# Hybrid RWKV-7 / S5 block: a 16-row RWKV inverse, readout of block 3 in halves, GLU of three blocks behind a norm

## Chip, cores and metric

One core of a Trainium2 chip runs the whole layer in one launch. The metric is the device time in microseconds; less is better. Engines are called PE (TensorE), DVE (VectorE), ACT (ScalarE), POOL (GpSimd) and SP (the queue that issues the DMAs here).

## What is computed

One layer over 2048 latent tokens and 256 context tokens, width 1024, all in float32. After an RMSNorm with modulation, one projection gives the inputs of two mixers: a bidirectional RWKV-7 (8 heads of 64) and a bidirectional diagonal S5 with a gated output (GLU). Their outputs are joined, projected, added to x; a second norm, a SwiGLU FFN (2816 wide) and a final norm follow. The recurrence of one RWKV head and direction is

```
sa    = state @ (-kk_t)
state = state * w_t + sa (kk_t * a_t)^T + v_t k_t^T
y_t   = state @ r_t
```

and the S5 output is `z * sigmoid(z @ glu_w + glu_b)` with `z = gelu(y)`. Context is scanned first, in each direction, and its last state is where the latent scan of that direction begins.

## The kernel before, in words

**RWKV in units.** A unit is 128 tokens of one direction, all eight heads, in two chunks of 64 tokens. Units 0 and 1 are context, 2 to 17 the latent tokens; direction 1 (backward in time) is run on context first, its state put aside in the tile `back`, then direction 0 runs whole, and then direction 1 takes its state from `back`: 36 units in all. `Rwkv.unit` has three parts.
- `prep` (L936 on) loads r, k and kk, makes the decayed tiles Q and BK, multiplies them per chunk (L992), masks the products, and copies the 32x32 diagonal blocks of the triangular matrices to AX and the blocks beside them to AY (L999). Q has two buffers, AX one.
- `inverse` (L1013 on) inverts 16 unit-triangular 64x64 matrices (eight heads, two chunks), each as two 32x32 blocks. AX is spread and transposed to AT (L1020, L1021), so that each partition holds a block's coefficients; then 31 steps of forward substitution, each a product (L1028) and a sum (L1030) over up to 76 elements a partition, on POOL or, where `dve` is true, on DVE. The result is transposed (L1033), copied (L1034) and transposed per quarter of the partitions into TW (L1037). Two rounds of 16 small products on PE (L1043 and L1050, called pz below), with ACT copies between (L1046, L1053), fill in the 32x32 block off the diagonal.
- `chain` (L1065 on) takes the state through a chunk: products with Q, with TW (L1081), with BT (L1090), the new state, and y (L1103, L1105, copied at L1111).

The PSUM pool `ph` has one buffer for tag `p`, which the products of the inverse and those of the chain take in turn.

**Tail.** Blocks are 512 latent tokens. `glu(b, put)` computes the S5 gate of a block in four column steps; each splits z and the weights into a high and a low float32r part, does 12 matmuls (L1218), and puts its product to the joined tile (`keep`, block 3) or to DRAM (`store`, blocks 2 to 0). `readout(b, put)` makes the RWKV output in eight steps, two halves of 256 tokens with four groups of 128 channels: head means (L1238), variances (L1283), transposes, bonus and gate. `outproj`, `norm` and `ffn` follow; an FFN has six splits, `SPLITS`, the first five of four column groups (L1400) and each ends in a `product` (L1324 to L1326, added to X on POOL at L1332).

**Order.** The input projections run block by block with the S5 pairs and units 2 to 12 of direction 0 between them, up to about 1390 us. Then the tail's pools open. Program order there: units 13 to 17 of direction 0 and 2 to 5 of direction 1, even ones with the loop on DVE, each followed by two steps of the GLU of block 3, a step that does nothing, and the GLUs of blocks 2, 1, 0; the rest of them between the steps of the readout of block 3; its output projection (upper half behind unit 14, lower half here); its norm; units 6 to 17; FFN splits 0 to 2 of block 3; then the RWKV pools close, and the readout, projection, norm and FFN of blocks 2, 1, 0 follow, FFN work of the block before beside them. Units 2 and 3 of direction 1 are the last 256 tokens of block 3, units 4 and 5 its first 256.

Program order sets priorities only. The framework orders the instructions of each engine when the kernel is built, from a simulated timeline: whatever is ready and has a buffer is placed, the earliest in the program first. On the chip every engine then runs its instructions in that fixed order.

Of the kernel before, what the change touches and what calls it, by code (L numbers as in the profile page):

```python
# [9 lines left out]
F32 = mybir.dt.float32  # L10
# [5 lines left out]
P = 128  # L16
# [34 lines left out]
def setup_consts(tc, pool, I):  # L51
# [13 lines left out]
    K["sel"] = pool.tile([P, 2], F32, name="sel")  # L65
# [20 lines left out]
def mod_group(tc, I, K, S, wt, st, fp, n, tag="f"):  # L86
# [15 lines left out]
    if sec in (2, 5):  # L102
        nc.tensor.matmul(pc[0:2, 0:P], K["sel"], rows, start=True, stop=True)
# [4 lines left out]
    else:  # L108
        nc.tensor.matmul(pc[:, 0:2], rows, K["sel"], start=True, stop=True)
# [12 lines left out]
class Front:  # L122


    def __init__(self, tc, I, K, S, p, p2, fp):
# [16 lines left out]
        for q in range(4):  # L142
            nc.vector.tensor_copy(K["sel"][32 * q:32 * q + 32], ident[32 * q:32 * q + 32, 32 * q:32 * q + 2])
# [668 lines left out]
class Rwkv:  # L812
# [4 lines left out]
    def __init__(self, tc, I, K, S, pool, pw, ph, nq=2, nb=4):  # L817
# [30 lines left out]
        self.back = r.tile([P, 4, 64], F32, name="back")  # L848
# [6 lines left out]
        lane = r.tile([P, 32, 8], F32, name="tmp")  # L855
        ev = r.tile([P, 4], F32, name="ev")
# [10 lines left out]
    def use(self, pool):  # L867

        TW = []
        for i in range(2):  # L870
            TW.append(pool.tile([P, 8, 64], F32, name="TW%d" % i))
            for q in (32, 96):
                self.nc.gpsimd.memset(TW[i][q:q + 32, :, 0:32], 0.0)
# [139 lines left out]
    def inverse(self, h, dve):  # L1013
# [8 lines left out]
        T = r.tile([P, 32, 8], F32, name="T")  # L1022
        act(T, self.TI, AF.Copy)
        tmp = r.tile([P, 32, 8], F32, name="tmp").rearrange("p a b -> p (a b)")
        for l in range(31):
            n, m = 31 - l, l // 4 + 1
            tv = tmp[:, 0:n * m].rearrange("p (a b) -> p a b", b=m)
            eng.tensor_tensor(tv, AT[:, l + 1:, l:l + 1].to_broadcast([P, n, m]), T[:, l:l + 1, 0:m].to_broadcast([P, n, m]),  # L1028
                              op=OP.mult)
            eng.tensor_tensor(T[:, l + 1:, 0:m], T[:, l + 1:, 0:m], tv, op=OP.add)  # L1030
# [515 lines left out]
```

## Time and profile before

| | |
|---|---|
| median of 3 runs | 3895.47 us (3886.15 to 3898.79) |
| profiled execution, its own time | 3900.97 us |
| its span, first to last instruction | 3899.3 us |
| mean granted TensorE clock | 0.888 of full |
| busy: PE | 3395.1 us (87%) |
| busy: DVE | 2430.7 us (62%) |
| busy: ACT | 1669.1 us (43%) |
| busy: POOL | 1740.9 us (45%) |
| DMA | 524.21 MB, 134 GB/s |

The profile is one execution. Busy times are of the whole span, and the stages differ, so shares are read by stretch. A line such as L1028 stands for all instructions that this line of the kernel issued. Float32 matmuls appear as two PE instructions each (16 products are x32), float32r matmuls as one. The granted clock is 1.0 at 2.4 GHz and 0.5 at 1.2 GHz.

### The profile page before, as it was taken

The page shows a single profiled execution, that of the slowest core. Times are in us where ns is not written, and L with a number is a line of the kernel's source. Part 1 is how long each engine was busy: PE and PEld are TensorE (multiplying, and loading weights), DVE is VectorE, ACT ScalarE, POOL GpSimd, SP SyncE. Part 2 cuts the span into 40 slices and gives each one's busy share as a digit, 9 for nine tenths or more (in the row PEclk, how much of TensorE's full clock was granted, in tenths as well). Part 3 has the DMA queues.
Part 4 walks back from the last instruction along what each step waited for, and adds up shares of the span by engine and source line. Part 5 has one row for each costly group of instructions (what it writes and reads, how often), then busy time and mean ns, then how long its engine had stood idle before and what let it go on. Part 6 is the DMA issues. An engine that isn't in the chain of part 4 may idle for free. (4 is left out here: it accounts for less than half of the span.)

```text
span 3899.3 us, 70208 instructions
## 1 busy us (share of the span) xinstructions
PE 3395.1 (87%) x25311; PEld 2810.8 (72%) x25311; DVE 2430.7 (62%) x4684; ACT 1669.1 (43%) x3696; POOL 1740.9 (45%) x3138
## 2 busy tenths in 40 slices
PE   5689877878888768767899999799999999999998
PEld 3567656656666547555778788688889888898887
DVE  7745677687787877655666655666444764454444
ACT  3577333324344345544554554444333433343333
POOL 3467437456757645447656663323212221231222
PEclk9789988888899868755699999799999999999999
DMA  7576766565475456512233333445333533334333
GB/s 186 169 223 173 224 191 204 151 215 159 141 222 154 131 132 145 128 49 83 82 99 106 97 95 94 142 133 149 105 101 98 164 107 103 103 95 128 102 101 94
DMA packets 767708, 524.21 MB, mean 134 GB/s; under 512 B 183760, under 2 KB 725076, under 8 KB 767360
## 3 DMA queue, kind: packets, MB, share of 16 engines
q1 hardware_dynamic: 767360, 519.72, 46.4%
q8 instruction: 200, 3.28, 0.3%
q14 instruction: 148, 1.21, 0.1%
HBM read 416.94 MB, written 102.62 MB: 133 GB/s over the span
## 5 line engine op out<-in xcount | busy, mean ns | idle before, releaser
L1332 POOL TENSOR_TENSOR X<-X,t 128x256 f32<-128x256 f32 x464 | 380.6, 849 | 963.9 <-DVE t L1329 959.6
L249 PE MATMUL pa<-HL,wq 128*128 128x512 f32 (+1 forms) x2136 | 592.4, 429 | 76.7 <-ACT wq L243 15.8
L249 PEld LDWEIGHTS pa<-HL,wq 128*128 128x128 f32 x2136 | 423.1, 221 | 189.3 <-ACT wq L243 19.6
L1028 POOL TENSOR_TENSOR tmp<-AT,T 128x60 f32<-128x60 f32 (+24 forms) x992 | 380.8, 384 | 243.1 <-DVE AT L1021 84.1
L1173 DVE TENSOR_TENSOR wl<-wr,wh 128x512 fp32r<-128x512 f32 x368 | 269.3, 733 | 282.1 <-PE f L1400 243.8
L1030 POOL TENSOR_TENSOR T<-T,tmp 128x60 f32<-128x60 f32 (+24 forms) x992 | 395.7, 399 | 69.5
L1173 DVE TENSOR_TENSOR vl<-vr,vh 128x256 fp32r<-128x256 f32 x480 | 252.3, 529 | 266.2 <-ACT vh L1172 265.5
L1172 ACT ACTIVATE wh<-wr 128x512 fp32r<-128x512 f32 x368 | 232.0, 631 | 418.4 <-PE f L1400 394.7
L1325 PE MATMUL f<-vl,gh 128*128 128x256 f32 x1408 | 397.4, 291 | 8.6 <-DVE vl L1173 8.1
L1400 PE MATMUL f<-H,wl 128*128 128x512 f32 x1408 | 390.0, 397 | 7.8 <-DVE wl L1173 7.6
L1400 PE MATMUL f<-H,wh 128*128 128x512 f32 x1408 | 390.3, 397 | 4.5 <-ACT wh L1172 4.4
L1400 PE MATMUL f<-L,wh 128*128 128x512 f32 x1408 | 391.9, 395 | 0.0
L1326 PE MATMUL f<-vh,gl 128*128 128x256 f32 x1408 | 390.4, 286 | 0.0
L1172 ACT ACTIVATE vh<-vr 128x256 fp32r<-128x256 f32 x480 | 198.6, 416 | 431.2 <-PE f L1326 369.1
L1324 PE MATMUL f<-vh,gh 128*128 128x256 f32 x1408 | 363.2, 290 | 3.4 <-ACT vh L1172 3.4
L282 DVE SCALAR_TENSOR_TENSOR acc<-zb,cw,acc 128x512 f32<-128x512 f32 (+2 forms) x384 | 323.4, 854 | 39.9 <-ACT acc L278 35.8
L1400 PEld LDWEIGHTS f<-H,wl 128*128 128x128 f32 x1408 | 261.8, 190 | 64.8 <-DVE wl L1173 9.3
L1400 PEld LDWEIGHTS f<-L,wh 128*128 128x128 f32 x1408 | 263.1, 189 | 57.8
L1400 PEld LDWEIGHTS f<-H,wh 128*128 128x128 f32 x1408 | 258.9, 189 | 59.1 <-ACT wh L1172 5.3
L1325 PEld LDWEIGHTS f<-vl,gh 128*128 128x128 f32 x1408 | 272.8, 194 | 20.1 <-DVE vl L1173 13.7
L1326 PEld LDWEIGHTS f<-vh,gl 128*128 128x128 f32 x1408 | 273.1, 194 | 2.5
L1324 PEld LDWEIGHTS f<-vh,gh 128*128 128x128 f32 x1408 | 255.2, 194 | 13.1 <-ACT vh L1172 5.3
(452 smaller groups left out, 6632.0 us busy)
## 6 DMA issues: line engine op xcount, KB each, us to landing
wr<-in_ffn_w_dram SPq DMA_DIRECT2D x352, 256.0 KB
vr<-in_ffn_w_dram SPq DMA_DIRECT2D x352, 128.0 KB
wq<-s_win SPq DMA_DIRECT2D x84, 512.0 KB
ld<-s_rkvk SPq DMA_DIRECT2D x36, 768.0 KB
raw<-in_w_in_dram SPq DMA_DIRECT2D x94, 256.0 KB
wq<-in_mod_w_dram SPq DMA_DIRECT2D x64, 256.0 KB
vr<-in_w_out_dram SPq DMA_DIRECT2D x128, 128.0 KB
gq<-s_gate SPq DMA_DIRECT2D x116, 128.0 KB
```

Source lines behind the costliest of these rows:

```text
L249: nc.tensor.matmul(pa[:, :nt], w[:, kc, :], H[4 * kh + kc][:, h, :nt].bitcast(F32R), start=kh + i + kc == 0, stop=kh == 1 and i == 2 and k ...
L282: nc.vector.scalar_tensor_tensor(ag, zb[:, i0 - 1 + a:i0 - 1 + a + nr, e:e + 64], tap(a, e), ag, op0=OP.mult, op1=OP.add)
L1028: eng.tensor_tensor(tv, AT[:, l + 1:, l:l + 1].to_broadcast([P, n, m]), T[:, l:l + 1, 0:m].to_broadcast([P, n, m]), op=OP.mult)
L1030: eng.tensor_tensor(T[:, l + 1:, 0:m], T[:, l + 1:, 0:m], tv, op=OP.add)
L1172: self.nc.scalar.activation(hi, x, AF.Copy)
L1173: self.nc.vector.tensor_tensor(lo, x, hi.bitcast(F32), op=OP.subtract)
L1324: mm(o, ah[:, js], vh, start=k == 0 and j % 2 == 0, stop=False)
L1325: mm(o, ah[:, js], vl, start=False, stop=False)
L1326: mm(o, al[:, js], vh, start=False, stop=k == n - 1 and j % 2 == 1)
L1332: nc.gpsimd.tensor_tensor(x, x, t[:, j], op=OP.add)
L1400: mm(p, a[:, kc, :], h[:, 4 * kh + kc, :], start=kh + i + kc == 0, stop=kh == 1 and i == 2 and kc == 3)
```

## The change

Four parts. **The inverse** now substitutes 16x16 blocks: 15 steps over two diagonal sub-blocks at once (up to 44 elements a partition), always on POOL for the units of the tail, which all get `dve` false. One transpose gives T2; a product with the mask MG spreads it to DN (normal) and a 128x512 transpose gives DT, both in the space of AT. 32 products (za, 16 rows each) multiply the AX block with DN, one DVE instruction masks the result and adds the unit diagonal (G), 32 products (zb, 64 columns) multiply with DT, and an ACT copy fills TW. Two small transposes make the TN that L1043's products read; those and the rest of the tail stay. za, zb and pz all take tag `p`. **`back`** moves to DRAM: two DMAs to store, two to load, in place of DVE copies. `sel` grows from 2 to 32 columns (it is the unit diagonal for G), MG is made at setup, and the zero fill of TW goes. **The readout of block 3** is called by halves: the second half behind unit 3, the first behind unit 5. **The GLUs of blocks 2 to 0** stand behind the norm of block 3, ahead of units 6 to 17.

```diff
+        self.MG = r.tile([P, 5], F32, name="MG")
+        for g in range(4):
+            nc.vector.tensor_reduce(self.MG[:, g:g + 1],
+                                    K["ident"].rearrange("p (h g c) -> p g h c", h=2, g=4)[:, g], mybir.AxisListType.XY, OP.add)
+        nc.vector.tensor_add(self.MG[:, 4:5], self.MG[:, 1:2], self.MG[:, 3:4])
...
-                nc.vector.tensor_copy(self.back[RH[par]], self.sv[RH[par], par])
+                nc.sync.dma_start(self.S["back"][RH[par]], self.sv[RH[par], par])
...
-                nc.vector.tensor_copy(self.sv[RH[par], par], self.back[RH[par]])
+                nc.sync.dma_start(self.sv[RH[par], par], self.S["back"][RH[par]])
...
-        for l in range(31):
-            n, m = 31 - l, l // 4 + 1
...
-        TN = tmp.rearrange("p (b l) -> p b l", l=32)
-        T2 = r.tile([P, 8, 4, 8], F32, name="T2")
-        nc.vector.transpose(T2.rearrange("p m e b -> p m (e b)"), T.rearrange("p i m -> p m i"))
-        act(TN.rearrange("p b (m e) -> p m e b", e=4), T2, AF.Copy)
-        for q in range(4):
-            o = 32 * (q % 2)
-            nc.vector.transpose(TW[32 * q:32 * q + 32, :, o:o + 32], TN[32 * q:32 * q + 32])
+        for l in range(15):
+            n, m = 15 - l, l // 4 + 1
+            tv = tmp[:, 0:2 * n * m].rearrange("p (s a b) -> p s a b", s=2, b=m)
+            co = bass.AP(tensor=AT.tensor, offset=AT.offset + 32 * (l + 1) + l, ap=[AT.ap[0], [528, 2], [32, n], [0, m]])
+            eng.tensor_tensor(tv, co, T[:, :, l:l + 1, 0:m].to_broadcast([P, 2, n, m]), op=OP.mult)
+            eng.tensor_tensor(T[:, :, l + 1:, 0:m], T[:, :, l + 1:, 0:m], tv, op=OP.add)
+        T2 = r.tile([P, 8, 4, 8], F32, name="T2")[:, 0:4]
+        nc.vector.transpose(T2.rearrange("p m e b -> p m (e b)"), T.rearrange("p s i m -> p m (s i)"))
+        fa = AT.rearrange("p a b -> p (a b)")
+        DN, DT = [fa[:, 512 * i:512 * i + 512].rearrange("p (b c) -> p b c", c=64) for i in range(2)]
+        nc.vector.tensor_tensor(DN.rearrange("p b (g c) -> p b g c", g=4),
+                                T2.rearrange("p m e b -> p b (m e)")[:, :, None, :].to_broadcast([P, 8, 4, 16]),
+                                self.MG[:, None, 0:4, None].to_broadcast([P, 8, 4, 16]), op=OP.mult)
+        nc.vector.transpose(fa[:, 512:1024], fa[:, 0:512])
+        za = self.ph.tile([P, 2, 8, 32], F32, name="p")
+        for b in range(8):
+            for q in range(4):
+                o = 32 * (q % 2)
+                mm(za[32 * q:32 * q + 32, 0, b, :], AX[0][32 * q:32 * q + 16, :, b], DN[32 * q:32 * q + 16, b, o:o + 32],
+                   start=True, stop=True)
+        G = r.tile([P, 8, 32], F32, name="T2")
+        nc.vector.scalar_tensor_tensor(G, za[:, 0], self.MG[:, 4:5], self.K["sel"][:, None, :].to_broadcast([P, 8, 32]),
+                                       op0=OP.mult, op1=OP.add)
+        zb = self.ph.tile([P, 8, 64], F32, name="p")
+        for b in range(8):
+            for q in range(4):
+                rq = slice(32 * q, 32 * q + 32)
+                mm(zb[rq, b, :], G[rq, b, :], DT[rq, b, :], start=True, stop=True)
+        act(TW, zb, AF.Copy)
...
+        for par in range(2):
+            r0 = 64 * par
+            nc.vector.transpose(TN[r0:r0 + 32], TW[r0:r0 + 32, :, 0:32])
...
-        for hf in range(2):
+        for hf in halves:
...
-            rest = chain(T.glu(3, T.keep), iter([None]), *[T.glu(b, T.store) for b in (2, 1, 0)])
+            first = T.glu(3, T.keep)
...
-                R.unit(h, h % 2 == 0, pe_add=True)
+                R.unit(h, False, pe_add=True)
                 for _ in range(2):
-                    next(rest, None)
+                    next(first, None)
                 if h == 14:
                     T.outproj(3, range(4, 8))
-            for _ in T.readout(3, T.keep):
-                next(rest, None)
-            run(rest)
+                if h in (3, 5):
+                    run(T.readout(3, T.keep, (1,) if h == 3 else (0,)))
             T.outproj(3, range(4))
             T.norm(3)
+            for b in (2, 1, 0):
+                run(T.glu(b, T.store))
```

## Rows read from the trace of the kernel before

**Rows 1.** Windows view by stage: us, then each engine's busy time; PEclk, DMA share, GB/s last
```profile
600.00:1390.00 790.00, 643.69 (x5600) 490.92 (x5599) 607.43 (x977) 306.55 (x692) 495.34 (x890) 0.85 0.56 169
1390.00:1800.00 410.00, 284.49 (x2988) 227.81 (x2988) 262.10 (x595) 202.24 (x480) 211.06 (x433) 0.70 0.47 113
1800.00:1962.00 162.00, 143.83 (x1154) 114.08 (x1154) 102.72 (x253) 75.42 (x202) 106.44 (x242) 0.64 0.27 73
1962.00:2430.00 468.00, 448.52 (x4041) 375.21 (x4043) 282.62 (x464) 235.91 (x522) 273.84 (x606) 0.96 0.35 101
2430.00:2620.00 190.00, 168.78 (x1102) 151.70 (x1099) 118.36 (x304) 85.07 (x226) 62.31 (x78) 0.87 0.43 126
2620.00:3899.30 1279.30, 1245.73 (x7361) 1098.49 (x7359) 662.25 (x1264) 456.59 (x984) 296.12 (x369) 0.99 0.38 113
```

**Rows 2.** Timeline: start, duration, engine, line; units 2, 4, 4 and 6 of direction 1
```profile
1682.86 0.86 PE L1105 MATMUL p<-Q,SV 64*64 64x64 f32 x16
...
1688.87 2.08 PE L992 MATMUL w<-Q,BK 64*128 64x128 f32 x16 [4.53 <-POOL Q L977]
...
1701.90 0.68 DVE L1020 COPY AT<-AX 128x1024 f32<-128x1024 f32 x1
...
1773.05 0.68 DVE L1020 COPY AT<-AX 128x1024 f32<-128x1024 f32 x1
```

**Rows 3.** Timeline: tail of unit 4's inverse, at the half clock
```profile
1729.44 0.65 DVE L1033 STREAM_TRANSPOSE T<-T 128x256 f32<-128x256 f32 x1
...
1732.41 1.20 PE L1043 MATMUL p<-tmp,AY 32*32 32x32 f32 x32
...
1737.25 1.06 PE L1050 MATMUL p<-TW,T 32*32 32x32 f32 x32
1738.35 0.76 ACT L1053 ACTIVATE TW<-p 32x256 f32<-32x256 f32 x2 [0.62 <-PE p L1050]
```

**Rows 4.** Groups by line, 1390 to 1800 us: busy us, mean ns, idle before
```profile
L1030 POOL TENSOR_TENSOR T<-T,tmp 128x60 f32<-128x60 f32 (+24 forms) x179 | 66.9, 374 | 12.8
L1028 POOL TENSOR_TENSOR tmp<-AT,T 128x60 f32<-128x60 f32 (+24 forms) x179 | 65.4, 366 | 58.8 <-DVE AT L1021 19.9 <-DVE TW L1037 19.4 <-PE p L1081 7.5
...
L1028 DVE TENSOR_TENSOR tmp<-AT,T 128x60 f32<-128x60 f32 (+24 forms) x124 | 31.9, 257 | 3.7
```

**Rows 5.** Groups by line, whole run: a VectorE product over 128x512
```profile
L1173 DVE TENSOR_TENSOR wl<-wr,wh 128x512 fp32r<-128x512 f32 x368 | 269.3, 733 | 282.1 <-PE f L1400 243.8 <-ACT wh L1172 31.1 <-ACT t L1340 2.2
```

**Rows 6.** Timeline of PE: small products at the full clock (two instructions each)
```profile
2310.61 1.18 PE L1043 MATMUL p<-tmp,AY 32*32 32x32 f32 x32
...
2317.15 0.69 PE L1050 MATMUL p<-TW,T 32*32 32x32 f32 x32
...
2321.85 0.68 PE L1081 MATMUL p<-R,TW 64*64 64x64 f32 x16
```

**Rows 7.** Timeline: from unit 5's y to the FFN of block 3
```profile
1789.01 0.77 ACT L1111 ACTIVATE YW<-p 64x256 f32<-64x256 f32 x2 [3.12 <-PE p L1105]
...
1800.30 1.22 PE L1238 MATMUL f<-yl,Cm 128*128 128x256 f32 x2 [0.28 <-POOL yl L1273]
...
1877.94 1.01 PE L1283 MATMUL f<-blk,yl 128*128 128x2 f32 x4
...
1931.49 0.28 PE L1326 MATMUL f<-vh,L 128*128 128x256 f32 x1
...
1961.87 1.20 PE L1400 MATMUL f<-H,wh 128*128 128x512 f32 x4
```

**Rows 8.** Windows view of L1218, the GLU's matmuls: PE, PEld, PEclk, DMA, GB/s
```profile
1390.00:1800.00 410.00, 60.67 (x192) 38.94 (x192) 0.70 0.47 113
```

**Rows 9.** Chain that ended last: FFN matmuls of 512 columns without a gap
```profile
3525.08 22.66 PE f L1400 x96
```

**Rows 10.** Timeline: FFN split 3 of block 3, and the last unit's inverse
```profile
2343.71 0.28 PE L1324 MATMUL f<-vh,gh 128*128 128x256 f32 x1
...
2414.22 0.76 ACT L1053 ACTIVATE TW<-p 32x256 f32<-32x256 f32 x2 [2.44 <-PE p L1050]
```

More of the change, by code (lines that the diff above doesn't have):

```diff
@@ L64, in setup_consts @@
     K["scp"] = pool.tile([P, 8, 32], F32, name="scp")
-    K["sel"] = pool.tile([P, 2], F32, name="sel")
+    K["sel"] = pool.tile([P, 32], F32, name="sel")
     return K
@@ L102, in mod_group @@
     if sec in (2, 5):
-        nc.tensor.matmul(pc[0:2, 0:P], K["sel"], rows, start=True, stop=True)
+        nc.tensor.matmul(pc[0:2, 0:P], K["sel"][:, 0:2], rows, start=True, stop=True)
         mb = st[0:1, P:2 * P]
@@ L108, in mod_group @@
     else:
-        nc.tensor.matmul(pc[:, 0:2], rows, K["sel"], start=True, stop=True)
+        nc.tensor.matmul(pc[:, 0:2], rows, K["sel"][:, 0:2], start=True, stop=True)
         o = VOFF["mod_b"] + n
@@ L142, in __init__ @@
         for q in range(4):
-            nc.vector.tensor_copy(K["sel"][32 * q:32 * q + 32], ident[32 * q:32 * q + 32, 32 * q:32 * q + 2])
+            nc.vector.tensor_copy(K["sel"][32 * q:32 * q + 32], ident[32 * q:32 * q + 32, 32 * q:32 * q + 32])
         self.eps = p.tile([P, 1], F32, name="eps")
@@ L847, in __init__ @@
         self.LT = r.tile([98, 2, 256], F32R, name="LT")
-        self.back = r.tile([P, 4, 64], F32, name="back")
         nc.vector.tensor_copy(self.LT[96:98], ones[96:98, None, 0:1].to_broadcast([2, 2, 256]))
@@ L1031, in inverse @@
-        TN = tmp.rearrange("p (b l) -> p b l", l=32)
-        T2 = r.tile([P, 8, 4, 8], F32, name="T2")
-        nc.vector.transpose(T2.rearrange("p m e b -> p m (e b)"), T.rearrange("p i m -> p m i"))
-        act(TN.rearrange("p b (m e) -> p m e b", e=4), T2, AF.Copy)
-        for q in range(4):
-            o = 32 * (q % 2)
-            nc.vector.transpose(TW[32 * q:32 * q + 32, :, o:o + 32], TN[32 * q:32 * q + 32])
+        T = r.tile([P, 32, 8], F32, name="T").rearrange("p a b -> p (a b)")[:, 0:128].rearrange("p (s i m) -> p s i m", s=2, m=4)
@@ new lines, in inverse @@
+        act(T, self.TI[:, None, 0:16, 0:4].to_broadcast([P, 2, 16, 4]), AF.Copy)
+        TN = r.tile([P, 8, 32], F32, name="tmp")
+        tmp = TN.rearrange("p a b -> p (a b)")
+        for l in range(15):
[4 more added lines that the diff above has]
+            eng.tensor_tensor(T[:, :, l + 1:, 0:m], T[:, :, l + 1:, 0:m], tv, op=OP.add)
@@ L1226, in glu, with readout @@
             yield
-    def readout(self, b, put):
+    def readout(self, b, put, halves=(0, 1)):
         nc, f1, S, K = self.nc, self.f1, self.S, self.K
@@ L1429 @@
            "zh": (12, P, 3, 64), "gate": (2, D), "wd": (32, 16, 496), "z": (512, 16, P),
-           "win": (14, 2, P, 2, 4, P), "hx": (3, 8, P, 2, 512), "s5t": (16, P, NTAB), "s5p": (16, P, 2, 2, 144), "s5d": (64, 16, 16), "y": (2, 512, NX), "pb": (2, 512, NX),
+           "win": (14, 2, P, 2, 4, P), "hx": (3, 8, P, 2, 512), "back": (P, 4, 64), "s5t": (16, P, NTAB), "s5p": (16, P, 2, 2, 144), "s5d": (64, 16, 16), "y": (2, 512, NX), "pb": (2, 512, NX),
            "cat": (D, NX)}
```

11 lines of the change are left out of this document (1 added, 10 removed).

## The prediction

> **What bounds the kernel now.** I read the windows view first, cut where the program's stages change [rows 1]. Four stretches matter. A (600 to 1390 us, input projections with 11 RWKV units beside them): no engine is full, PE 644 of 790 us, DVE 607, POOL 495. B (1390 to 1962 us, its first two windows: units 13 to 17 and 2 to 5, then readout, output projection and norm of block 3): PE is busy 428 of 572 us, and at a mean granted clock of 0.70 and 0.64 (1.0 is 2.4 GHz, 0.5 is 1.2 GHz), so it mostly waits. C (1962 to 2430 us, FFN of block 3 with the rest of the units): PE 449 of 468 us at 0.96; PE is the bound. Behind 2430 us PE is nearly full again, apart from 21 us idle at clock 0.87 in the first 190 us. So time saved in B is saved at the end, and TensorE work added from 1962 us on is paid in full.
>
> Then the timeline of B, for what sets the pace of a unit [rows 2]. The last products on a Q tile (L1105, unit 2) end at 1683.7; the same slot is then refilled for unit 4, its products (L992) start 1688.9, and unit 4's AT copy comes at 1701.9; that of unit 6 comes at 1773.1. Q has two buffers, so this is a loop over two units: 71.2 us, 35.6 a unit. In it lie 18.2 us from the last product to the AT copy, 2 us of copy and transpose, the 31-step loop to 1729.4 [rows 3] (25.5 us for unit 4), the tail of the inverse to 1739.1 (9.7), and the rest, 15.8 us of state chain. TensorE's, ScalarE's and VectorE's steps stand in it one behind the other, each waiting for the one before.
>
> **The change, part by part.** One execution is taken: span 3899.3 us, 3901.0 in all, 5.5 above the median 3895.5. The sum is made against 3901.0 and its difference carried to the median.
>
> *Inverse loop.* 31 pairs of instructions become 15. In B a pair on POOL costs 366 + 374 ns, on DVE about twice 257 ns [rows 4], so a loop holds 22.9 us of instructions on POOL (odd units) and 15.9 on DVE (even units). Afterwards all units take POOL: 15 pairs, at most 11.1 us, as the operands are smaller. Other work stands between the pairs: unit 4's 15.9 us on the busier DVE took 25.5; for POOL I add a third, so 30 us elapsed before and 14 after. Over five POOL units (16 less) and four DVE units (11.5 less) that is 14 us less latency a unit.
>
> *Inverse tail.* Out go a transpose, an ACT copy, and four small transposes; the old ones, with the two products pz that stay, took the 9.7 us of [rows 3]. In come a smaller transpose, a DVE product over 128x512 (0.73 us by a row of that size [rows 5]), a 128x512 transpose beside it, 32 matmuls (za), a DVE pass over 128x256, 32 matmuls (zb), an ACT copy of 128x512 and two small transposes, all in sequence but one. Nearest rows for the matmuls, at the full clock [rows 6]: 16 products of 32x32 with strided weights 1.18 us (74 ns each), with contiguous weights 0.69 us (43 ns), eight of 64 columns 0.68 us (85 ns). za reads strided weights: 32 x 74 = 2.4 us; zb has 64 columns: 1.4 to 2.7 us. That makes 3.8 to 5.1 us; those rows use two quarters of the array in turn, the new ones four, so the lower end is half of it, 1.9. I take 3.5, nearer to the rows than to the half. The tail grows by about 7.5 us: 0.7 + 3.5 + 0.4 + 0.6 + 0.9 of new work, about 1.3 of clock and 1.4 of five engine hops, less the 1.3 of transpose and copy that go.
> Latency per unit: -14 + 7.5 = -6.5 us, in a loop over two units, so -3.3 us a unit; nine units in B: -30 us. Bounds: 0 (the pace stays) and -72 (nine times 8 us, if half the loop's saving arrives and the tail is hidden).
>
> *Readout in halves.* Unit 5's last y copy starts at 1789.0, the readout's first product stands at 1800.3 and the statistics of its eighth and last step at 1877.9, so a step takes 77.6 / 7 = 11 us; the output projection's last product is at 1931.5, the FFN's first at 1961.9 [rows 7]. Four of the eight steps now run beside units 4 and 5: 44 us, of which I take -40 (bounds -30 and -45), and give back 8 us for their DVE and POOL work in the units' queues, since they now stand ahead of units 4 and 5. Behind the readout the output projection is late next, unchanged.
>
> *GLU of blocks 2 to 0.* 192 GLU matmuls keep PE busy 60.7 us in B [rows 8], three quarters belong to the moved blocks, with their splits on ACT and DVE and 12 POOL products ahead of the units in each queue, and 24 loads of z and 12 of weights on SP. Out of the units' way: -12 us in B (bounds 0 and -25). Where do they go? 144 matmuls at 22.66 us for 96 [rows 9] are 34 us of PE at the full clock, paid whole if they run in C. But the order of instructions comes from a planner that fills idle engines with ready work of later stages: products of FFN split 3 start at 2343.7, ahead of the last unit's inverse at 2414.2 [rows 10]. z lies ready from the start of B, so most of the GLU can fill gaps in B. I take +8 us (bounds 0 and 34).
>
> A rule weighs against this part. PE's granted clock in B is already low, and the 16 products of L1050 take 1.06 us there against 0.69 in C [rows 3, 6]. The Trainium skill (TensorE: Matmul & The Clock Gate, Part 1) says that the array's half rate is its default state and that activity is what releases it; dense GLU matmuls taken out of B would leave its small products at the half rate for longer. By the row B's gain stays as above; by the rule the four units 15, 16, 17 and 2 would each lose some 3 us of it, a third of about 9 us of products (1.06 / 0.69 less one, spread over them, is a half at most), 12 us in all, and the sum would be 3863. The row only shows both rates, not which of them the emptier stretch gets.
>
> *TensorE's added work in C.* 12 units x 3.5 us = +42 us (bounds 12 x 1.9 = 23 and 12 x 5.1 = 61), since PE is the bound.
>
> *Behind C.* Units that end sooner leave more FFN work to cover the readout of block 2, where PE idled 21 us and ran at clock 0.87 (another 22 us lost): -20 us (bounds 0 and -35).
>
> *A.* 15 units add 52 us to a PE that has 146 us idle of 790 in the stretch shown, and take 16 pairs x 0.74 = 12 us a unit off POOL. I take 0 (bounds -40 and +52).
>
> *Costed at nothing.* The `back` state goes through DRAM instead of a DVE copy: the reload waits for nothing but its slot, and the first use is unit 2's chain, behind a whole inverse; without that cover it is one DMA round trip of a few us, once. `sel` is wider by 30 columns, once; MG is five small DVE instructions at setup.
>
> Sum: -30 - 12 - 40 + 8 + 8 + 42 - 20 + 0 = -44 us: 3857 against the profiled 3901, 3851 against the median. I say 3850.
>
> **Rivals.**
> *One PSUM bank decides (no change).* Tag p has one buffer; za and zb take it, then the old pz products, then two chain tiles. Now pz holds it 6.7 us (1732.4 to 1739.1 [rows 3]) and the chain nearly 16, so 22.5 of 35.6 us a unit; with za and zb at 3 each, 28.5 of 32. If turns collide, the unit's pace stays: -30 falls away, and half of -20: about 3891. For it: the share. Against: inverse tail and chain of neighbouring units fall naturally one behind the other. Chance 0.14.
> *TensorE pays everywhere (slower).* If A is as good as bound by PE (or by the coupling of PE and DVE), it pays its 52 us in full, and the GLU runs in C, +26 more: -44 + 78 = +34, 3929. It decides against the change once A and the GLU together cost 44 us more than I took. For it: PE and DVE are both at about 80% in A, and the clock is 0.85. Against: PE has gaps of 18%. Chance 0.23.
> *A gains too.* If the latency of units sets A's pace, 11 units x 3.3 us and the relief on POOL give another 45 us: 3805. For it: POOL is busy 495 of 790 us there, half of it in loops (11 x 22.9). Against: PE and DVE stand at about 80% and can hardly be filled further. Chance 0.18.
> That the planner leaves the GLU where it was would be a change that does not do what it says; it is the +0 end of that term.
>
> **How the numbers follow.** My forecast has 0.45 and is faster, A's gain 0.18 too: 0.63. No change 0.14, slower 0.23. About 0.3%, 12 us, is what a measurement can tell from none. The forecast's own range, from its terms' bounds taken partly, is 3810 to 3885. With the rivals: 3785 to 3925, which leaves out the far half of the last two.
>
> **What would show it.** Right: AT copies of units 4 and 6 about 64 us apart; the loop of one unit 12 to 15 us; the FFN's first matmul near 1890 instead of 1962; the units' end before 2400; za and zb together 3 to 4 us in C. Wrong: AT copies still 71 us apart (bank), block 4's projections ending later than 1390 by 20 us or more (PE in A), or GLU matmuls in one dense run behind the norm (the +34 end). If B shrinks by less than 60 us, the forecast falls.

## The result, and the profile after

The change is slower: 3928.7 us (median of 5 runs, 3920.24 to 3936.33) against 3895.5, a ratio of 1.0086 (1.0062 to 1.0111). The forecast was 3850 us, with a range that ends at 3925. The profiled execution of the changed kernel took 3920.2 us (span 3918.5).

The windows of the changed kernel, cut as [rows 1]:

```profile
600.00:1390.00 790.00, 671.83 (x6901) 512.80 (x6901) 609.24 (x964) 298.01 (x677) 332.33 (x535) 0.86 0.56 170
1390.00:1800.00 410.00, 294.19 (x4143) 239.93 (x4145) 226.68 (x405) 190.22 (x470) 170.93 (x373) 0.65 0.32 88
1800.00:1962.00 162.00, 135.79 (x1513) 111.24 (x1510) 104.70 (x217) 79.99 (x209) 68.59 (x139) 0.75 0.35 89
1962.00:2430.00 468.00, 439.58 (x5058) 359.79 (x5057) 275.18 (x472) 245.04 (x535) 170.57 (x333) 0.94 0.43 115
2430.00:2620.00 190.00, 187.60 (x1265) 173.26 (x1264) 120.11 (x274) 79.54 (x193) 61.58 (x79) 0.99 0.42 121
```

POOL falls from 495 to 332 us in A. PE rises by 28 us there, where the forecast's 3.5 us a unit would make 38 for the stretch's 11 units. B's first window has a low mean clock as before, a little lower (0.65, was 0.70). C, where PE was busy 448.5 of 468 us at 0.96, is less full (439.6 us at 0.94).

The timeline of the changed kernel (start, duration, engine, line): unit 4's AT copy, first and last step of its loop, then its products on PE; unit 6's AT copy; za and zb of a unit in C; the FFN's first matmul; the last unit's inverse.

```profile
1698.08 0.68 DVE L1022 COPY AT<-AX 128x1024 f32<-128x1024 f32 x1
1700.19 0.25 POOL L1033 TENSOR_TENSOR tmp<-AT,T 128x30 f32<-128x30 f32 x1 [14.20 <-DVE AT L1023]
1712.26 0.20 POOL L1034 TENSOR_TENSOR T<-T,tmp 128x8 f32<-128x8 f32 x1
1714.59 1.21 PE L1049 MATMUL p<-AT,AX 16*32 16x32 f32 x64 [2.39 <-DVE AT L1040]
...
1718.85 1.06 PE L1058 MATMUL p<-AT,T 32*32 32x64 f32 x28
1724.72 1.22 PE L1263 MATMUL f<-yl,Cm 128*128 128x256 f32 x2 [4.80 <-POOL yl L1298]
...
1729.07 0.86 PE L1058 MATMUL p<-AT,T 32*32 32x64 f32 x22
...
1731.87 0.64 PE L1058 MATMUL p<-AT,T 32*32 32x64 f32 x12
...
1786.34 0.68 DVE L1022 COPY AT<-AX 128x1024 f32<-128x1024 f32 x1
...
2039.87 1.20 PE L1425 MATMUL f<-H,wh 128*128 128x512 f32 x4
...
2229.21 1.19 PE L1049 MATMUL p<-AT,AX 16*32 16x32 f32 x64
...
2233.51 1.10 PE L1058 MATMUL p<-AT,T 32*32 32x64 f32 x64
...
2376.47 0.76 ACT L1078 ACTIVATE TW<-p 32x256 f32<-32x256 f32 x2 [0.22 <-PE p L1075]
```

The loop is 12.3 us long where it was 25.5 [rows 3], and the last unit's inverse ends 38 us earlier than in [rows 10]. But units 4 and 6 stand 88.3 us apart, not 64 (71.2 before, [rows 2]): unit 4's 32 products zb, which take 1.1 us in one piece in C, are pulled apart over 13.7 us by the readout's products (L1263), which stand between them in PE's fixed order; the first of them waits 4.80 us for POOL. And the FFN of block 3 begins at 2039.9 instead of 1961.9 [rows 7], behind the GLUs of blocks 2 to 0, as the windows of L1243 alone (PE, PEld, PEclk, DMA, GB/s) show, where [rows 8] had 192 matmuls beside the units:

```profile
1389.00:1922.00 533.00, 14.51 (x48) 9.24 (x48) 0.67 0.32 86
1922.00:2040.00 118.00, 47.66 (x144) 29.30 (x144) 0.78 0.66 139
```

So 144 matmuls sit in one run of 118 us behind the norm. PE is busy 91 of these 118 us in all.

Three of the forecast's signs of being right came true, and the time was lost all the same: the loop of 12.3 us, the units' end before 2400 us, and B shorter by over 60 us (1389 to 1922 us up to the end of the norm, where it was 1367 to 1962 up to the FFN). The loss lies behind the units. Here are the windows from the last unit's inverse to the end, before and after, and then the FFN's matmuls (L1400, now L1425) between the FFN's start and that inverse:

```profile
2415.00:3899.30 1484.30, 1429.51 (x8579) 1262.01 (x8577) 787.05 (x1578) 548.17 (x1221) 358.44 (x447) 0.97 0.39 114
2377.00:3918.50 1541.50, 1504.40 (x9113) 1334.77 (x9112) 831.74 (x1645) 577.29 (x1278) 372.99 (x468) 0.99 0.39 117
```

```profile
1962.00:2415.00 453.00, 217.82 (x887) 163.95 (x888) 0.96 0.35 101
2040.00:2377.00 337.00, 143.20 (x576) 106.05 (x576) 0.98 0.35 100
```

Fewer FFN matmuls are done when the units end (576, were 887), so PE has 75 us more to do behind them, and that stretch takes 57 us more. Of the 38 us that the units gained nothing is left: these two executions lie 19 us apart in span.

### The profile page after: what moved, and what is told of

Read it like the earlier page. It is cut to its first block, busy times and chain, and to the rows that moved or that the text cites. A ratio compares the mean times of both kernels' runs of the same rounds, so it can differ in the third digit from the quotient of the medians.

```text
span 3918.5 us, 78312 instructions
## 1 busy us (share of the span) xinstructions
PE 3453.8 (88%) x29919; PEld 2871.4 (73%) x29919; DVE 2413.2 (62%) x4473; ACT 1672.3 (43%) x3702; POOL 1347.4 (34%) x2230
## 5 line engine op out<-in xcount | busy, mean ns | idle before, releaser
L249 PE MATMUL pa<-HL,wq 128*128 128x512 f32 (+1 forms) x2136 | 593.8, 430 | 84.0 <-DMA wq<-s_win 25.7
L249 PEld LDWEIGHTS pa<-HL,wq 128*128 128x128 f32 x2136 | 423.5, 222 | 189.6 <-DMA wq<-s_win 23.0
L1425 PE MATMUL f<-H,wl 128*128 128x512 f32 x1408 | 388.8, 396 | 8.1 <-DVE wl L1198 8.1
L1425 PE MATMUL f<-L,wh 128*128 128x512 f32 x1408 | 391.1, 394 | 0.0
L1425 PE MATMUL f<-H,wh 128*128 128x512 f32 x1408 | 389.1, 396 | 1.7 <-ACT wh L1197 1.7
L282 DVE SCALAR_TENSOR_TENSOR acc<-zb,cw,acc 128x512 f32<-128x512 f32 (+2 forms) x384 | 313.1, 828 | 21.8 <-ACT acc L278 17.5
L1425 PEld LDWEIGHTS f<-H,wl 128*128 128x128 f32 x1408 | 262.0, 189 | 64.3 <-DVE wl L1198 9.4
L1425 PEld LDWEIGHTS f<-L,wh 128*128 128x128 f32 x1408 | 262.1, 189 | 56.9 <-issue 0.2
L1425 PEld LDWEIGHTS f<-H,wh 128*128 128x128 f32 x1408 | 258.4, 189 | 53.8 <-ACT wh L1197 2.5
L1033 POOL TENSOR_TENSOR tmp<-AT,T 128x36 f32<-128x36 f32 (+2 forms) x540 | 179.2, 332 | 316.4 <-DVE AT L1023 248.8
L1034 POOL TENSOR_TENSOR T<-T,tmp 128x36 f32<-128x36 f32 (+2 forms) x540 | 188.8, 350 | 39.6
```

Of the source, the lines that this page charges most:

```text
L249: nc.tensor.matmul(pa[:, :nt], w[:, kc, :], H[4 * kh + kc][:, h, :nt].bitcast(F32R), start=kh + i + kc == 0, stop=kh == 1 and i == 2 and k ...
L282: nc.vector.scalar_tensor_tensor(ag, zb[:, i0 - 1 + a:i0 - 1 + a + nr, e:e + 64], tap(a, e), ag, op0=OP.mult, op1=OP.add)
L1033: eng.tensor_tensor(tv, co, T[:, :, l:l + 1, 0:m].to_broadcast([P, 2, n, m]), op=OP.mult)
L1034: eng.tensor_tensor(T[:, :, l + 1:, 0:m], T[:, :, l + 1:, 0:m], tv, op=OP.add)
L1425: mm(p, a[:, kc, :], h[:, 4 * kh + kc, :], start=kh + i + kc == 0, stop=kh == 1 and i == 2 and kc == 3)
```

## The experiments

Each time is followed by its ratio to the kernel before on the same chip, with the 95% interval; 1% is 39 us. The front is the program up to the last input projection (L249).

### One part of the change at a time

`inv_only` has the new inverse everywhere and the tail in the old order; `tail_only` the old inverse and the new order; `glu_beside` is the changed kernel with the GLUs back beside the units; `front_old` is it with the old inverse in the front's 15 units.

```diff
 inv_only: the changed kernel, tail in the order of before
-                if h in (3, 5):
-                    run(T.readout(3, T.keep, (1,) if h == 3 else (0,)))
+            for _ in T.readout(3, T.keep):
+                next(rest, None)
...
 tail_only: the kernel before, tail in the order of the change
 glu_beside: the changed kernel
-            first = T.glu(3, T.keep)
+            rest = chain(T.glu(3, T.keep), iter([None]), *[T.glu(b, T.store) for b in (2, 1, 0)])
...
 front_old: the changed kernel
-        self.inverse(h, dve)
+        (self.inverse_old if self.old else self.inverse)(h, dve)
...
```

> The new inverse alone (all units, loops on POOL), the tail in the old order. Theory 'front pays': the inverse costs the front stretch about 20 us (block 4's projections end near 1389 instead of 1368) and gives back less than that later: 3895 to 3920. Theory 'GLU placement': the inverse is a gain and the order of the tail is the whole loss: 3850 to 3875.

> The old inverse with the new order of the tail (readout of block 3 in halves, GLU of blocks 2 to 0 behind its norm). Theory 'GLU placement': the norm ends 40 us sooner, but the FFN of block 3 starts only behind the GLU run, over 80 us after the norm; end 3900 to 3930. Theory 'front pays': the order is a gain: 3850 to 3875. In both block 4's projections end at 1368.

> The changed kernel with the GLU of blocks 2 to 0 back beside the units; new inverse and readout halves stay. Theory 'GLU placement': the FFN of block 3 starts within 5 us of the norm again; 30 to 60 us less than the changed kernel: 3870 to 3900. Theory 'front pays': no difference beyond 12 us: 3916 to 3940.

> The changed kernel with the old inverse for the 15 units of the front (0, 1 twice, 2 to 12); everything from unit 13 on as changed. Theory 'front pays': block 4's projections end at 1368 again, 20 to 25 us less: 3904 to 3909. Theory 'GLU placement' alone: 3920 to 3935.

Measured: `inv_only` 3901.1 us, 1.0023 (1.0013 to 1.0033); `tail_only` 3912.9, 1.0051 (1.0033 to 1.0069); `glu_beside` 3915.7, 1.0061 (1.0047 to 1.0076); `front_old` 3917.1, 1.0066 (1.0049 to 1.0083). Neither theory holds throughout: `inv_only` lies in the range of 'front pays' and `tail_only` in that of 'GLU placement', `glu_beside` is some 10 us under the change where the second theory had 30 to 60, and `front_old` falls between both. The tail's order alone is a loss of 20 us, with the old inverse too; from `inv_only` to `glu_beside` (halves) it is 15, from there to the change (GLU) 10. The new inverse everywhere is a small loss (9 us), and by `front_old` the front holds about 8 of the change's 33 us.

### The new inverse behind the front only

`inv_tail` leaves everything up to the front's end as it was, makes the masks there, and gives only the 21 units behind it the new inverse, in the old order. `small_parts` is the kernel before with the change's `sel`, MG at setup and `back` in DRAM, and nothing else. The two others are the changed kernel with the GLUs between the FFN's splits, and with two buffers for AX, which za reads, so that the next unit's ACT copies need not wait for it.

```diff
 inv_tail
+            R.masks16()
+            R.new = True
             rest = chain(T.glu(3, T.keep), ...
-                R.unit(h, h % 2 == 0, pe_add=True)
+                R.unit(h, False, pe_add=True)
 glu_between
-            for b in (2, 1, 0):
-                run(T.glu(b, T.store))
...
-            run(T.ffn(3, SPLITS[:3]))
+            for b, split in zip((2, 1, 0), SPLITS[:3]):
+                run(T.ffn(3, [split]))
+                run(T.glu(b, T.store))
 ax_two
-        AX = kp.tile([P, 32, 8], F32, name="AX"), ...
+        AX = kp.tile([P, 32, 8], F32, name="AX", bufs=2), ...
```

> The old inverse and the old code up to the end of the front; only the nine units beside block 4's attention and the twelve units after them take the 16-row inverse, in the old order of the tail. Theory 'the front pays, the tail gains': the front's last projections end at 1365 to 1370 us as before, the stretch from there to the end of the second norm takes 1207 us as with the new inverse everywhere (1231 before), 3868 to 3880 us. Rival 'whatever touches the units moves the front's order too': the front ends 15 us or more later, 3888 to 3900 us.

> The kernel before with the small parts of the change alone: the selector 32 wide, the five columns of masks, the saved state sent to DRAM and back in place of a copy on DVE. Theory 'the small parts move the front's order': the front's last projections end 15 us or more later than 1368, 3905 to 3915 us. Rival 'they cost nothing', as forecast: 1363 to 1373, 3888 to 3899 us.

> The changed kernel with the GLU of blocks 2, 1 and 0 set between the FFN's splits of block 3 instead of in one run behind the norm. Theory 'the dense GLU run wastes TensorE': the FFN starts at about 1925 us, right behind the norm, and the 30 to 45 us that TensorE lost in that run to waits and half clock come back in part, 3885 to 3905 us. Rival 'the waits only move': the GLU's DVE and ACT steps hold up the FFN in the same measure, 3915 to 3932 us.

> The changed kernel with two buffers in place of one for AX, which the first products of the new inverse read, so that the next unit's copies into AX need not wait for them. Theory 'AX holds back the next unit': copies into AT of successive units stand closer by 5 to 8 us each in B, the end of the units behind the front 30 to 60 us earlier than 2377, 3895 to 3915 us. Rival 'the pace is set elsewhere' (DVE, the order on TensorE, the bank of products): the distance stays, 3918 to 3935 us.

Measured: `inv_tail` 3854.9 us, 0.9894 (0.9877 to 0.9911), 41 us faster than before, better than either expectation and the fastest of all kernels here; `small_parts` 3896.2, 1.0005 (0.9995 to 1.0016); `glu_between` 3899.5, 1.0015 (1.0004 to 1.0027), 28 us under the change; `ax_two` 3905.9, 1.0029 (1.0017 to 1.0041), 22 under it; the last two lie in the range of the first theory each. `inv_tail` in the timeline: the AT copies of unit 13, then of units 2, 4 and 6 of direction 1 (between the last two the end of unit 4's inverse), the last y copy of unit 5, the FFN's first matmul, the last unit's inverse:

```profile
1388.21 0.68 DVE L1073 COPY AT<-AX 128x1024 f32<-128x1024 f32 x1
...
1644.57 0.68 DVE L1073 COPY AT<-AX 128x1024 f32<-128x1024 f32 x1
...
1711.79 0.68 DVE L1073 COPY AT<-AX 128x1024 f32<-128x1024 f32 x1
...
1742.47 0.76 ACT L1129 ACTIVATE TW<-p 32x256 f32<-32x256 f32 x2
...
1777.39 0.68 DVE L1073 COPY AT<-AX 128x1024 f32<-128x1024 f32 x1
...
1792.58 0.77 ACT L1187 ACTIVATE YW<-p 64x256 f32<-64x256 f32 x2
...
1945.62 1.09 PE L1476 MATMUL f<-H,wh 128*128 128x512 f32 x4
...
2364.01 0.76 ACT L1129 ACTIVATE TW<-p 32x256 f32<-32x256 f32 x2 [0.28 <-PE p L1126]
```

Units 4 and 6 are 65.6 us apart, near the forecast's loop over two units (71.2 less 6.5, about 64). But that holds for units 2 to 6 only. In the kernel before, the AT copies of units 13 and 2 are these:

```profile
1386.71 0.68 DVE L1020 COPY AT<-AX 128x1024 f32<-128x1024 f32 x1
...
1632.39 0.68 DVE L1020 COPY AT<-AX 128x1024 f32<-128x1024 f32 x1
```

The five steps from unit 13 to unit 2 take 256 us in `inv_tail` and took 246 before; the four from there to unit 6 take 133 and took 141. So unit 5 copies its last y at 1792.6 us, no earlier than before (1789.0, [rows 7]): over B's nine units the shorter inverse has gained nothing. That the FFN starts 16 us earlier (1945.6, was 1961.9) comes about behind unit 5. The windows of `inv_tail`, from the front's last projection to the norm of block 3, and from there to the norm of block 2:

```profile
1364.00:1944.00 580.00, 449.65 (x5758) 364.07 (x5756) 345.76 (x647) 279.29 (x691) 254.60 (x514) 0.73 0.41 104
1944.00:2566.00 622.00, 604.32 (x6302) 516.05 (x6302) 393.54 (x743) 312.83 (x724) 222.24 (x415) 0.98 0.38 109
```

PE's busy time times the granted clock is about the work that PE did, in us at the full clock: 328 us in the first stretch and 592 in the second. The rest of each stretch, 252 and 30 us, was lost to waits and the half clock. These four numbers are the measure for the next runs. The clock is the mean of the whole stretch, so they are good to some 5 us.

`small_parts` misses in an odd way. Its front does end late, as one theory said: the last projection matmul (L249, the second time of the pair behind the durations) starts 27 us later than before. L249 from 1120 us on, in the kernel before and then in `small_parts`:

```profile
L249 PE MATMUL pa<-HL,wq x344: 387/396/797, 1119.6 to 1367.1; 128*128 128x512 f32 x172
```

```profile
L249 PE MATMUL pa<-HL,wq x349: 388/397/797, 1119.8 to 1394.6; 128*128 128x512 f32 x175
```

but the time is that of before. A few instructions at setup give the framework another order of all that follows, and the traces show it: on POOL and ACT `small_parts` runs its operations in another sequence than the kernel before from 171 and 177 us on, while `inv_tail` keeps the old one up to 1198 and 1217 us. With the old inverse the delay is caught up behind the front.

### What the tail's order does, and what the front costs, apart from each other

On top of `inv_tail`: the change's whole tail order; its readout halves alone; two buffers for AX (with `back` in DRAM, for room). And the new inverse in the front alone, with the small parts.

```diff
 inv_tail_order, inv_tail_halves: inv_tail
-            for _ in T.readout(3, T.keep):
-                next(rest, None)
+                if h in (3, 5):
+                    run(T.readout(3, T.keep, (1,) if h == 3 else (0,)))
 inv_tail_order besides
+            for b in (2, 1, 0):
+                run(T.glu(b, T.store))
             for h in range(6, 18):
 inv_front: the new inverse everywhere, up to
+            R.old = True
             rest = chain(T.glu(3, T.keep), ...
```

> The kernel of inv_tail (16-row inverse behind the front only, 3854.9) with the changed order of its tail: readout of block 3 in halves beside units 3 and 5, GLU of blocks 2 to 0 in one run behind the norm. Theory 'each part has a price of its own': the order costs what it cost with the old inverse (19 us, 3895 to 3913), so 3872 to 3885. Rival 'the order costs more with the faster units': it costs the 62 us that lie between the two kernels that have the old inverse in front only, 3910 to 3920.

> The kernel of inv_tail with the readout of block 3 in halves beside units 3 and 5 alone; the GLU stays beside the units. Theory 'the halves are a loss': 3866 to 3875 (they cost 15 us between the two kernels with the new inverse everywhere). Rival, as forecast, 'the halves save 32 us': 3823 to 3840.

> The 16-row inverse in the front's fifteen units alone, the old one behind, the tail in the old order. Theory 'in the front the added work on TensorE is paid in full': 3925 to 3940 (3893.5 and the 46 us between the new inverse everywhere and the new inverse behind the front). Rival 'A costs nothing', as forecast: 3890 to 3900.

> The kernel of inv_tail with two buffers for AX; the room for it comes from sending the saved state to DRAM and back, as the change does. Theory 'AX holds back the next unit' (the second buffer gave 23 us in the changed kernel): 3825 to 3845. Rival 'in the old order of the tail something else paces the units': 3850 to 3862.

Measured: `inv_tail_order` 3892.8 us, 1.0000 (0.9989 to 1.0010); `inv_tail_halves` 3867.6, 0.9935 (0.9924 to 0.9947); `inv_front` 3900.9, 1.0024 (1.0013 to 1.0035); `inv_tail_ax` 3858.0, 0.9908 (0.9892 to 0.9923). So the order takes back all of `inv_tail`'s 41 us: the halves 16 (as the first theory had it), the GLU run 25; the whole lies between both expectations. The front's inverses with the small parts cost 9 us, 7 more than the small parts alone: near the rival, far from the 46 that the other theory carried over. A second AX, with `back` in DRAM, gives nothing here (the front ends at 1364 us as in `inv_tail`); what it gave in the changed kernel was not a general price of AX, whose copies wait 5.9 us for za there in all of B.

The same two stretches, `inv_tail_halves`:

```profile
1365.00:1921.00 556.00, 428.02 (x5332) 347.72 (x5333) 323.81 (x614) 264.74 (x650) 235.03 (x469) 0.72 0.41 104
1921.00:2578.00 657.00, 625.20 (x6727) 532.12 (x6728) 413.89 (x776) 340.62 (x773) 241.99 (x459) 0.97 0.37 107
```

and `inv_tail_order`, with the GLU run between them:

```profile
1364.00:1881.00 517.00, 402.72 (x5233) 329.07 (x5233) 299.82 (x580) 243.49 (x617) 215.43 (x460) 0.68 0.33 89
1881.00:2004.00 123.00, 91.03 (x974) 68.31 (x972) 70.08 (x112) 59.56 (x131) 49.21 (x95) 0.76 0.62 128
2004.00:2589.00 585.00, 572.28 (x5845) 491.77 (x5842) 366.64 (x697) 302.16 (x676) 209.81 (x373) 0.99 0.40 114
```

With the halves, B is 24 us shorter, but PE's work in it is 308 us in place of 328: some 20 of the 24 us were work that now stands behind B, and only a few were waiting. Behind B that work is paid, and 51 us are lost there in place of 30. With the whole order, B is 63 us shorter, 54 of them work (274); the GLU run then takes 123 us for 69 of work. What B loses hardly shrinks (252, 248, 243 us), whatever is moved in it or out of it; behind B the loss grows from 30 to 51 and 72.

The GLU does stand in the units' way, by the room that it takes. Unit 2's AT copy in `inv_tail_halves`, and then in `inv_tail_order`, where the GLU of three blocks is gone from the units ahead of it:

```profile
1638.80 0.68 DVE L1073 COPY AT<-AX 128x1024 f32<-128x1024 f32 x1
```

```profile
1603.54 0.68 DVE L1073 COPY AT<-AX 128x1024 f32<-128x1024 f32 x1
```

That is 35 us, about as much as the work taken out of B (308 less 274).

### Which part of the small parts, and B against C

`inv_tail_mg` is `inv_tail` with MG's five instructions at setup; `inv_tail_small` with all small parts. `inv_b` returns to the old inverse for the twelve units behind the norm. `inv_tail_dve` leaves the even units' loops in B on DVE.

```diff
 inv_tail_mg: inv_tail
+        self.MG = r.tile([P, 5], F32, name="MG")
...
         ev = r.tile([P, 4], F32, name="ev")
 inv_b: inv_tail
+            R.new = False
             for h in range(6, 18):
 inv_tail_dve: inv_tail
-                R.unit(h, False, pe_add=True)
+                R.unit(h, h % 2 == 0, pe_add=True)
```

> The kernel of inv_tail (3854.9; front unchanged, its projections end at 1364) with one thing moved: the five small VectorE instructions that make the masks MG stand at the setup of the RWKV, as in the change, and not behind the front. They are under 1 us of work each; what they change is the framework's order of the front's instructions on every engine. Theory 'the moved order has a price of its own, hidden by the old inverse and not by the new': the front ends at 1385 to 1395, 3872 to 3885. Rival 'five small instructions cost nothing': 3850 to 3860.

> All small parts of the change (selector, masks at setup, saved state through DRAM), the old inverse in the front, the 16-row inverse behind it, the tail in the old order: between inv_only (3901) and this lie the fifteen front units alone. Theory 'the moved order': 3872 to 3885, so that the front's own inverses cost about 22 of the 46 us. Rival 'the front's inverses cost it all': 3855 to 3863.

> The kernel of inv_tail with the 16-row inverse in the nine units of B only, the old inverse in the twelve units beside the FFN of block 3. By the forecast's terms B alone is -30 (3864) and the twelve units add 42 less 20 (so this kernel would be 22 us faster than inv_tail, 3833). Rival, from inv_tail's profile: the added work in C displaces idle and half-clock time, and the twelve units gain about half of the 39 us: 3868 to 3880.

> The kernel of inv_tail with the even units of B keeping their substitution loop on VectorE, as before, in place of POOL. Theory 'the loop is off the path by now': within 6 us of inv_tail, 3849 to 3861. Rival 'POOL is the bound with all loops on it': faster, 3835 to 3848.

Measured: `inv_tail_mg` 3860.4 us, 0.9916 (0.9903 to 0.9929); `inv_tail_small` 3876.1, 0.9964 (0.9953 to 0.9976); `inv_b` 3859.4, 0.9921 (0.9909 to 0.9932); `inv_tail_dve` 3867.1, 0.9937 (0.9925 to 0.9949), some 12 to 17 us slower than `inv_tail`, which neither theory had: in this order the short loops are better on POOL. MG alone costs 5 to 9 us; all small parts cost 27 us, as the theory of the moved order said, though `small_parts` had cost nothing.

`inv_b` says that B alone is worth 31 us, and the twelve units of C another 10, by a difference whose intervals just touch. Neither expectation was this; the forecast's +22 for them is out. Its window against that of `inv_tail` from the FFN's start to the norm of block 2, first `inv_b`, then `inv_tail`:

```profile
1946.00:2572.00 626.00, 588.32 (x5011) 501.14 (x5011) 374.82 (x721) 303.63 (x703) 329.60 (x691) 0.95 0.37 107
```

```profile
1946.00:2566.00 620.00, 602.32 (x6273) 514.27 (x6272) 391.99 (x740) 312.01 (x722) 220.71 (x409) 0.98 0.38 110
```

Work rises from 559 to 590 us, and the loss falls from 67 to 30: the added products took the place of waits and of half clock.

The 31 us for B are not where the forecast had them. The last y copy of unit 5 in `inv_b` comes when it came before (1789.01, [rows 7]):

```profile
1789.30 0.77 ACT L1187 ACTIVATE YW<-p 64x256 f32<-64x256 f32 x2 [3.12 <-PE p L1181]
```

The FFN starts 16 us earlier than before, and the rest comes behind that, where both kernels have the old inverse; why, no run tells.

`inv_tail_small` and `inv_only` differ in the fifteen inverses of the front (and the zero fill of TW that the old one needs), and lie 23 us apart. Yet their fronts end within 1 us of each other, and the difference lies in B, first `inv_tail_small`, then `inv_only`:

```profile
1398.00:1955.00 557.00, 445.08 (x5553) 357.46 (x5550) 327.28 (x612) 271.31 (x671) 244.16 (x487) 0.72 0.42 105
```

```profile
1397.00:1981.00 584.00, 444.83 (x5666) 362.04 (x5667) 337.26 (x630) 274.44 (x682) 251.07 (x501) 0.71 0.41 103
```

The same program behind the front, the same busy time and nearly the same clock, 27 us more: what is left to differ is the order of the instructions, and on every engine the two traces list B's operations in different sequences. The delay is there at unit 2, whose AT copy comes at 1656.7 and 1686.4 us; 8 of the 27 us come back behind B.

### Two last runs

The GLU between the splits, on `inv_tail` (edit as in `glu_between`, readout whole), and `inv_tail_mg` with `back` in DRAM besides.

```diff
 inv_tail_mg_back: inv_tail_mg
-                nc.vector.tensor_copy(self.back[RH[par]], self.sv[RH[par], par])
+                nc.sync.dma_start(self.S["back"][RH[par]], self.sv[RH[par], par])
```

> The kernel of inv_tail with the readout of block 3 whole, as before, but the GLU of blocks 2 to 0 neither beside the units of B nor in one run behind the norm: one GLU behind each of the FFN's first three splits. By the runs so far, moving the GLU behind the norm cost 25 us and spreading it between the splits gave 29 back: 3845 to 3856 if these add. Rival 'the GLU is best where it fills the idle time of B': 3860 to 3875.

> The kernel of inv_tail with the masks at setup and the saved state through DRAM: the small parts without the selector. Alone they cost 5.5 us (masks) and at most 3 us (state through DRAM, with two buffers for AX). Theory 'prices add': 3858 to 3866. Rival 'together they make another order of the front': like all small parts (3876), front's projections ending at 1390 or later, 3870 to 3882.

Measured: `inv_tail_between` 3875.6 us, 0.9961 (0.9947 to 0.9975): the GLU is best beside the units of B, as the rival had it; the dense run cost 25 us, spreading it 26. `inv_tail_mg_back` 3892.8, 0.9999 (0.9987 to 1.0010): 41 us over `inv_tail`, for five short DVE instructions that stand earlier and four DMAs in place of copies, beyond either expectation, and more than with all small parts. In the profiled executions it is 28 us; its front ends 29 us later than that of `inv_tail`. Here are, in this order, `inv_tail` and `inv_tail_mg_back`:

```profile
L249 PE MATMUL pa<-HL,wq x336: 388/397/797, 1120.2 to 1363.9; 128*128 128x512 f32 x168
```

```profile
L249 PE MATMUL pa<-HL,wq x353: 388/397/796, 1119.7 to 1392.5; 128*128 128x512 f32 x177
```

and its later stretches are as long as those of `inv_tail` (581 and 615 us against 580 and 622), so the front's delay reaches the end:

```profile
1393.00:1974.00 581.00, 451.02 (x5633) 365.33 (x5635) 342.14 (x638) 274.65 (x683) 256.75 (x514) 0.70 0.41 103
1974.00:2589.00 615.00, 596.79 (x6301) 508.23 (x6300) 393.52 (x743) 312.58 (x724) 223.18 (x414) 1.00 0.38 111
```

## Why the prediction was wrong

Along one path of single steps, each the difference of two ratios times 3893 us (good to 5 to 11 us by their intervals), the change is made up as follows:

| step | forecast | measured | between |
|---|---|---|---|
| new inverse, units of B | -30 | -31 | before, `inv_b` |
| new inverse, units of C, and behind | +42 - 20 | -10 | `inv_b`, `inv_tail` |
| small parts | 0 | +27 | `inv_tail`, `inv_tail_small` |
| new inverse in the front (A) | 0 | +23 | `inv_tail_small`, `inv_only` |
| readout in halves | -40 + 8 | +15 | `inv_only`, `glu_beside` |
| GLU moved | -12 + 8 | +10 | `glu_beside`, the change |

The sum is +34, as measured (by the ratio, 33). The forecast's terms failed at "time saved in B is saved at the end", which the readout's halves and the GLU rest on, at the added TensorE work in C that was "paid in full", and at the small parts' cost of nothing. The single rows are no larger than the 5 to 41 us that another order of nearly the same work costs (`inv_tail_mg` to `inv_tail_mg_back` against `inv_tail`), so a row is a price on this path and not that of a mechanism by itself.

- **Inverse loop and tail: right. The pace of nine units: wrong, and its -31 us luck.** The loop takes 12.3 us (12 to 15 forecast). From unit 4's AT copy to the end of its inverse it is 31.4 us in `inv_tail` (1711.8 to 1743.2) and was 37.2 (1701.9 to 1739.1), so -5.8 us, where -6.5 was forecast. The step that failed is the next one, "nine units in B: -30": the pace was read from units 2 to 6 and carried over to units 13 to 17, which have the GLU beside them. These did not speed up, and the ninth unit ended no earlier. The -31 of `inv_b` came about behind unit 5, by a way that the forecast did not have. The bank rival falls: the bank of tag `p` takes za and zb besides, and units 2 to 6 still came closer together.
- **TensorE's added work in C: wrong, in sign.** The products are cheaper, 1.19 + 1.10 = 2.3 us a unit and not 3.5, so the bill is 28 us and not 42. And the step "PE is the bound", by which that work was "paid in full", failed: by busy time times clock, [rows 1] still hold 37 us of loss in C (468 less 431) beside the 43 behind it (190 less 147) that the forecast counted for its -20, and quicker units filled both.
- **Readout in halves: the term that failed most.** The step "Four of the eight steps now run beside units 4 and 5" (-40 + 8) took B's shortening for time saved. B did shorten (24 us in `inv_tail_halves`), but some 20 of that was work pushed into C, and C loses 21 us more to waits and half clock. In the change, zb stands split around the readout's products. The 8 us given back for queues were too few: units 4 and 6 stand 22.7 us further apart in the change than in `inv_tail`. The sentence "time saved in B is saved at the end" is where this began.
- **GLU: the sum's -4 was +10, and +25 on top of `inv_tail`.** The step that failed is "most of the GLU can fill gaps in B": the planner put its 144 matmuls into one run of 118 us behind the norm, the forecast's own sign of the +34 end. Out of the units' way it gave B more than the 12 us forecast (unit 2 comes 35 us earlier), but that was the GLU's own work; B's loss fell by 5 us (248 to 243). In the change the FFN starts behind that run, and the FFN matmuls that the units had covered follow behind the units, 75 us of PE more.
- **The clock rule named in the forecast.** With the GLU out, B's mean granted clock fell to 0.68 in `inv_tail_order` from 0.72 in `inv_tail_halves`, and in the change to 0.65 in its first window from 0.70 before, where other parts changed too. That is the way the Trainium skill says (TensorE: Matmul & The Clock Gate, Part 1), where activity is what releases the half rate. The 12 us for units 15, 16, 17 and 2 are not seen: these units came sooner without the GLU. No run separates the clock's time from that of the waits.
- **"Costed at nothing" was the other hole.** The parts are small as work, but each changes the order in which the framework lays out everything behind it. `inv_tail` and the four kernels that add one or more of the small parts to it (`inv_tail_ax`, `inv_tail_mg`, `inv_tail_small`, `inv_tail_mg_back`) lie from 0.9894 to 0.9999. With the old inverse the same parts cost 2 us; why that order is caught up there and not with the new inverse, no run tells.
- **A, and the rival that came closest in time.** "TensorE pays everywhere" gave 3929, but not for its reason. A's PE work rose by 31 us (578 less 547, busy times clock in the windows) in the same window of 790 us, and alone the front's inverses cost 7 us; the +23 of the table is a difference of order in B. Forecast as 52 us paid in full or 0, they cost a little. The last projection starts 21 us later in the change than before (1388.6, was 1367.1), but in `small_parts` 27 us later, without the added work. The forecast's sign for this was set from 1390 us, where the projections were taken to end, and so could not show it. L249 in the change:

```profile
L249 PE MATMUL pa<-HL,wq x372: 388/397/793, 1121.3 to 1388.6; 128*128 128x512 f32 x186
```

The prices depend on the path: the tail's order costs 20 us with the old inverse, 25 with the new one everywhere, 41 with the new one behind a front left as it was. In no pair of kernels here is it a gain. `inv_tail`, the new inverse behind the front in the old tail, is 41 us faster than the kernel before and some 74 faster than the change.

## What to carry to other kernels

A stretch that gets shorter because work was moved out of it has saved nothing: compare busy time times clock in the stretch and behind it before a shortening is booked. Read the pace of a chain in every part of the stretch that it is carried over to, not in one pair of its steps. Work that fills the waits of a latency-bound chain was best left there in these runs. And where a planner fixes the order at build time, a change that adds a few instructions early can move the time by 40 us, as much as the change under study; put such parts where the order ahead of them stays, and judge an edit by more than one order.

## What the runs showed of the hardware

64 instructions of 16x32 products in four quarters of the array take 1.19 us at the full clock, as long as 32 instructions of 32x32 in two quarters did [rows 6]: 37 ns a product in place of 74, with strided weights. In the trace the new instructions start in groups of four and the old ones in groups of two; both kinds of group follow each other about every 62 ns. The 16 rows in place of 32 are not the reason: zb, with 32 rows and 64 columns in four quarters, takes 1.10 us. The forecast had put this at its lower end. The Trainium skill (TensorEngine Tiling (Array Packing), Key Properties) says that tiles of the array load and multiply independently of each other; the trace agrees for four quarters against two.
